# Binary cross-entropy with an 8-bit target: clip, negate and Ln by halves, and the last full store from GpSimd

## The chip, the cores and the metric

The kernel runs on one core of a Trainium2 chip. The metric is the device time of one execution in microseconds (us): the median of three runs before the change is 1889.43 us (1887.55 to 1890.08). One more execution was taken by the hardware profiler; it took 1891.86 us, and all rows below are from it.

The core's engines are called as in the profile: DVE (VectorE), ACT (ScalarE), POOL (GpSimd), SP (SyncE). TensorE does nothing here. Transfers between HBM and the on-chip memory run on 16 DMA engines, fed by queues of the engines that issue them.

## The reference

```python
"pred": np.random.uniform(0.01, 0.99, (8192, 8192)).astype(np.float32),
"target": np.random.randint(0, 2, (8192, 8192)).astype(np.float32),
...
eps = 1e-7
pred = np.clip(pred, eps, 1 - eps)
return -(target * np.log(pred) + (1 - target) * np.log(1 - pred))
```

Two inputs of 256 MiB are read and one of 256 MiB is written. Since the target is 0 or 1, the kernel computes the same with one logarithm: with p clipped, |t - 1 + p| is p where t is 1 and 1 - p where t is 0; the result is minus the Ln of it.

## The kernel before, in words

**Tiling.** The flat arrays are cut into chunks of 128 partitions by w columns: a first chunk of 8192 columns, 33 chunks of WIDE = 15232 columns, and a tail of three, a, b and c, of 6208, 6208 and 1024 columns. The last full chunk is called z (z = 33 when the first chunk is 0).

**Buffers.** `ring_p` holds three chunks of pred in float32; the result is computed in place there, so a slot is used again only when the store of its chunk has landed. `ring_t` has one slot only, in uint8: the target is cast from float32 to uint8 by the DMA that loads it. The next target can so be issued only when both halves of `merge` have read the present one. The tail's three chunks lie side by side in one slot of each ring.

**Steps for one chunk k.** `clip` (line 85, DVE): maximum and minimum with constants. `merge` (lines 91 and 94): DVE adds t - 1 to p, then ACT takes Abs. `log` (line 98, ACT): Ln. `negate` (line 102, DVE): times -1. Clips, merges and negates all stand in DVE's one queue, Abs and Ln in ACT's.

**DMA queues.** `load_p` (line 70) and `load_t` (line 73) are issued from GpSimd, except for the first p, which ACT issues. `store` (line 79) issues from GpSimd for chunks below z, and from SP for z, a, b and c. The store of c is cut into three by rows (108, 12, 8).

**Order.** The order is written out by hand (`manual_schedule`); within each engine's queue the instructions stand as in the source. A turn of the main loop for chunk k: merge in two halves, issue t of k+1, Ln, negate, clip of chunk k+1, store of k, issue p of k+2. So on GpSimd each turn has three issues: t (waits for the merges), store (waits for the negate), p (waits for the store that used the slot before). In the turn of chunk 1 alone, Ln and negate are by halves. After the loop come the merges of z with Ln by halves, the issue of all loads of a, b and c, and the rest of the tail, with clip and negate in the order of the source: negate z (half 0), clip a, negate z (half 1), store z, merge a, clip b, merge b, negate a, store a, clip c, merge c, negate b, store b, negate c, store c.

Of the kernel before, what the change touches and what calls it, by code (L numbers as in the profile page):

```python
# [1 line left out]

# [4 lines left out]

EPS = 1e-7

WIDE = 15232  # L10
SLOTS = 3
TAIL = (6208, 6208, 1024)
ROWS = (108, 12, 8)


@with_exitstack
def kernel(
    ctx: ExitStack,
    tc: tile.TileContext,
    pred: bass.AP,  # L20
    target: bass.AP,
    out: bass.AP,
):
    nc = tc.nc
    fp32 = mybir.dt.float32
    low = mybir.dt.uint8
    Alu = mybir.AluOpType
    Act = mybir.ActivationFunctionType
    P = nc.NUM_PARTITIONS

    R, C = pred.shape
    total = R * C // P
    rest = total - sum(TAIL)
    n = rest // WIDE
    first = rest - n * WIDE
    assert 0 < first <= WIDE and n > 4 and sum(TAIL) <= WIDE
    spots = [(first, 0)]
    spots += [(WIDE, k % SLOTS * WIDE) for k in range(1, n + 1)]
    c = (n + 1) % SLOTS * WIDE
    for w in TAIL:  # L40
        spots.append((w, c))
        c += w
    n = len(spots)
    z = n - 1 - len(TAIL)
    starts = [sum(w for w, _ in spots[:k]) * P for k in range(n)]

    pool = ctx.enter_context(tc.tile_pool(name="rings", bufs=1))
    ring_p = pool.tile([P, SLOTS * WIDE], fp32, name="ring_p", tag="ring_p")
    ring_t = pool.tile([P, WIDE], low, name="ring_t", tag="ring_t")
    warm = pool.tile([1, 8], fp32, name="warm", tag="warm")  # L50

    def chunk(ap, k):
        flat = ap.rearrange("r c -> (r c)")
        w = spots[k][0]
        return flat[starts[k] : starts[k] + w * P].rearrange("(p w) -> p w", p=P)

    def cols(ring, k, part, c):
        w = spots[k][0]
        i, m = part
        return ring[:, c + i * w // m : c + (i + 1) * w // m]  # L60

    def p_of(k, part=(0, 1)):
        return cols(ring_p, k, part, spots[k][1])

    def t_of(k, part=(0, 1)):
        return cols(ring_t, k, part, spots[k][1] % WIDE)

    def load_p(k):
        queue = nc.scalar if k == 0 else nc.gpsimd
        queue.dma_start(out=p_of(k), in_=chunk(pred, k))  # L70

    def load_t(k):
        nc.gpsimd.dma_start(out=t_of(k), in_=chunk(target, k))  # L73

    def store(k):
        queue = nc.sync if k >= z else nc.gpsimd
        r = 0
        for rows in ROWS if k == n - 1 else (P,):
            queue.dma_start(out=chunk(out, k)[r : r + rows, :], in_=p_of(k)[r : r + rows, :])  # L79
            r += rows  # L80
        assert r == P

    def clip(k, *part):
        p = p_of(k, *part)
        nc.vector.tensor_scalar(  # L85
            out=p, in0=p, scalar1=EPS, scalar2=1 - EPS, op0=Alu.max, op1=Alu.min
        )

    def merge(k, *part):
        p, t = p_of(k, *part), t_of(k, *part)  # L90
        nc.vector.scalar_tensor_tensor(  # L91
            out=p, in0=t, scalar=1.0, in1=p, op0=Alu.subtract, op1=Alu.add
        )
        nc.scalar.activation(out=p, in_=p, func=Act.Abs)  # L94

    def log(k, *part):
        p = p_of(k, *part)
        nc.scalar.activation(out=p, in_=p, func=Act.Ln)  # L98

    def negate(k, *part):  # L100
        p = p_of(k, *part)
        nc.vector.tensor_scalar(out=p, in0=p, scalar1=-1.0, scalar2=None, op0=Alu.mult)  # L102

    halves = (0, 2), (1, 2)
    with tc.manual_schedule():
        load_p(0)
        load_t(0)
        load_p(1)
        nc.vector.memset(warm, 1.0)  # L109
        nc.scalar.activation(out=warm, in_=warm, func=Act.Ln)  # L110
        clip(0)
        for k in range(z):
            for h in halves:
                merge(k, h)
                if k == 1:
                    log(k, h)
            load_t(k + 1)
            if k == 1:
                for h in halves:
                    negate(k, h)  # L120
            else:
                log(k)
                negate(k)
            clip(k + 1)
            store(k)
            if k + 2 <= z:
                load_p(k + 2)
        for h in halves:
            merge(z, h)
            log(z, h)  # L130
        a, b, c = range(z + 1, n)
        for j in a, b, c:
            load_p(j)
            load_t(j)
        negate(z, halves[0])
        clip(a)
        negate(z, halves[1])
        store(z)
        merge(a)
        log(a)  # L140
        clip(b)
        merge(b)
        log(b)
        negate(a)
        store(a)
        clip(c)
        merge(c)
        log(c)
        negate(b)
        store(b)  # L150
        negate(c)
        store(c)


# [1 line left out]
_INS = ['pred', 'target']  # L156
_OUTS = [((8192, 8192), 'float32')]


# [23 lines left out]
```

## Time and profile before

| | |
|---|---|
| median of three runs | 1889.43 us (1887.55 to 1890.08) |
| the profiled execution | 1891.86 us |
| its span (first to last instruction) | 1889.9 us |
| DVE busy | 1109.2 us (59%), 148 instructions |
| ACT busy | 897.3 us (47%), 112 instructions |
| POOL busy | 296.8 us (16%), 110 instructions |
| HBM read and written | 536.87 MB and 268.44 MB, 426 GB/s over the span |
| store, p and t of a full chunk, from issue to landing (median) | 28.3, 38.6 and 37.6 us |

The last row is the time that a transfer takes including its time in the queue. A row of the timeline has the start in us, the duration in us, the engine (with a q where it is the engine's sequencer that issues), the line, the operation, and in brackets the idle time before it with what ended it. In the stretches of the DMA share, each row has the stretch, its length, busy time and instructions of DVE, ACT and POOL, the granted TensorE clock, the busy share of the DMA engines and GB/s.

### The profile page before, as it was taken

What the parts mean: (1) busy time and instruction counts of PE and PEld (TensorE: products, weight loads), DVE (VectorE), ACT (ScalarE), POOL (GpSimd) and SP (SyncE); (2) the same over time, 40 slices, a digit from 0 to 9 for tenths busy, and PEclk for the clock granted to TensorE, in tenths of its full rate; (3) what the DMA queues carried; (4) which work ended last, traced back from release to release, by engine and by line L of the source; (5) the groups of instructions that cost most, each with busy time, mean ns of one, the idle gap of its engine ahead of it and who ended that gap; (6) DMA issues with size and microseconds to landing.
All of it is one profiled execution on the core that took longest, in us unless ns stands there. A gap on an engine that the chain in (4) does not pass through costs nothing.

```text
span 1889.9 us, 528 instructions
## 1 busy us (share of the span) xinstructions
DVE 1109.2 (59%) x148; ACT 897.3 (47%) x112; POOL 296.8 (16%) x110
## 2 busy tenths in 40 slices
DVE  3656655555666555456665555666555556665573
ACT  3553444555444455554444555444445554444564
POOL 0111111101111111011111101111111011111100
DMA  9999999999999999999999999999999999999997
GB/s 297 295 351 302 300 313 302 309 356 351 325 310 308 310 306 325 355 343 306 306 312 310 307 356 356 340 310 310 310 308 310 351 356 322 308 312 306 294 347 290
DMA packets 16003, 604.01 MB, mean 320 GB/s; under 512 B 1792, under 2 KB 1920, under 8 KB 2432
## 3 DMA queue, kind: packets, MB, share of 16 engines
q0 software_dynamic: 15264, 585.11, 97.1%
q1 hardware_dynamic: 592, 14.68, 1.8%
q10 hardware_dynamic: 144, 4.19, 0.6%
q14 instruction: 3, 0.02, 0.0%
HBM read 536.87 MB, written 268.44 MB: 426 GB/s over the span
## 4 chain that ended last, share of the span: by engine, by line
DMA 67%; issue 27%; DVE 3%; ACT 2%; POOL 0%; POOLq 0%; DVEq 0%
DMA ring_t<-in_target_dram 66%; DVE ring_p L91 2%; DMA ring_p<-in_pred_dram 1%; ACT ring_p L98 1%; ACT ring_p L94 1%; DVE ring_p L102 0%; POOL out_dram L79 0%; DVE ring_p L85 0%; DVEq L178 0%; POOL ring_p L70 0%; POOLq L73 0%; POOLq L79 0%; DVEq L91 0%
## 5 line engine op out<-in xcount | busy, mean ns | idle before, releaser
L94 ACT ACTIVATE ring_p<-ring_p 128x7616 f32<-128x7616 f32 (+3 forms) x71 | 451.3, 6356 | 976.5 <-DVE ring_p L91 976.5
L102 DVE TENSOR_SCALAR ring_p<-ring_p 128x15232 f32<-128x15232 f32 (+4 forms) x39 | 279.2, 7162 | 647.1 <-ACT ring_p L98 647.1
L91 DVE SCALAR_TENSOR_TENSOR ring_p<-ring_t,ring_p 128x7616 f32<-128x7616 uint8 (+3 forms) x71 | 554.3, 7847 | 101.6 <-DMA ring_t<-in_target_dram 101.5
L98 ACT ACTIVATE ring_p<-ring_p 128x15232 f32<-128x15232 f32 (+4 forms) x39 | 444.8, 11406 | 1.2
L79 POOL DMA_DIRECT2D out_dram<-ring_p x33 | 258.2, 7826 | 876.8 <-DVE ring_p L102 876.8
L85 DVE TENSOR_SCALAR ring_p<-ring_p 128x15232 f32<-128x15232 f32 (+3 forms) x37 | 278.7, 7533 | 19.5 <-DMA ring_p<-in_pred_dram 19.5
L73 POOL DMA_DIRECT2D ring_t<-in_target_dram x37 | 19.7, 532 | 638.9 <-DVE ring_p L91 638.1
L70 POOL DMA_DIRECT2D ring_p<-in_pred_dram x36 | 19.0, 528 | 0.0
L110 ACT ACT_TABLE_LOAD x1 | 1.3, 1283 | 1.1 <-PEq L167 1.1
L109 DVE MEMSET warm<- 1x8 f32 x1 | 0.1, 65 | 0.8 <-PEq L167 0.8
L110 ACT ACTIVATE warm<-warm 1x8 f32<-1x8 f32 x1 | 0.2, 207 | 0.0
L167 POOL MEMSET const-float32-0.0<- 128x1 f32 x1 | 0.1, 99 | 0.2 <-issue 0.2
L167 POOL MEMSET const-bfloat16-1.0<- 128x1 bf16 x1 | 0.1, 101 | 0.0
L167 POOL MEMSET const-float32-1.0<- 128x1 f32 x1 | 0.1, 98 | 0.0
L167 POOL MEMSET const-uint8-127<- 128x1 uint8 x1 | 0.1, 98 | 0.0
## 6 DMA issues: line engine op xcount, KB each, us to landing
ring_p<-in_pred_dram POOLq DMA_DIRECT2D x33, 7616.0 KB, 38.6
out_dram<-ring_p POOLq DMA_DIRECT2D x32, 7616.0 KB, 28.3
ring_t<-in_target_dram POOLq DMA_DIRECT2D x33, 1904.0 KB, 37.6
out_dram<-ring_p SPq DMA_DIRECT2D x1, 7616.0 KB, 28.2
ring_p<-in_pred_dram POOLq DMA_DIRECT2D x2, 3104.0 KB, 29.6
out_dram<-ring_p SPq DMA_DIRECT2D x2, 3104.0 KB, 9.1
ring_p<-in_pred_dram ACTq DMA_DIRECT2D x1, 4096.0 KB, 19.7
out_dram<-ring_p POOLq DMA_DIRECT2D x1, 4096.0 KB, 19.7
```

Source lines behind the costliest of these rows:

```text
L70: queue.dma_start(out=p_of(k), in_=chunk(pred, k))
L73: nc.gpsimd.dma_start(out=t_of(k), in_=chunk(target, k))
L79: queue.dma_start(out=chunk(out, k)[r : r + rows, :], in_=p_of(k)[r : r + rows, :])
L85: nc.vector.tensor_scalar(out=p, in0=p, scalar1=EPS, scalar2=1 - EPS, op0=Alu.max, op1=Alu.min)
L91: nc.vector.scalar_tensor_tensor(out=p, in0=t, scalar=1.0, in1=p, op0=Alu.subtract, op1=Alu.add)
L94: nc.scalar.activation(out=p, in_=p, func=Act.Abs)
L98: nc.scalar.activation(out=p, in_=p, func=Act.Ln)
L102: nc.vector.tensor_scalar(out=p, in0=p, scalar1=-1.0, scalar2=None, op0=Alu.mult)
L109: nc.vector.memset(warm, 1.0)
L110: nc.scalar.activation(out=warm, in_=warm, func=Act.Ln)
L167: nc = _bacc.Bacc("TRN2", target_bir_lowering=False, num_devices=1)
```

## The change

The function `log` goes; its Ln is now the last step of `merge`, so it is done right behind the Abs of the same piece: by halves in the loop, whole in the tail, where the pieces are whole. In the loop, negate and clip are called for each half in place of once for the chunk, for the first clip too. The order of the steps in the source is otherwise kept. In `store`, the test `k >= z` becomes `k > z`: the store of z is issued from GpSimd, behind all loads of the tail in its queue; a, b and c stay on SP.

```diff
     def store(k):
-        queue = nc.sync if k >= z else nc.gpsimd
+        queue = nc.sync if k > z else nc.gpsimd
...
         nc.scalar.activation(out=p, in_=p, func=Act.Abs)
-
-    def log(k, *part):
-        p = p_of(k, *part)
         nc.scalar.activation(out=p, in_=p, func=Act.Ln)
...
-        clip(0)
+        for h in halves:
+            clip(0, h)
         for k in range(z):
             for h in halves:
                 merge(k, h)
-                if k == 1:
-                    log(k, h)
             load_t(k + 1)
-            if k == 1:
-                for h in halves:
-                    negate(k, h)
-            else:
-                log(k)
-                negate(k)
-            clip(k + 1)
+            for h in halves:
+                negate(k, h)
+            for h in halves:
+                clip(k + 1, h)
             store(k)
...
         for h in halves:
             merge(z, h)
-            log(z, h)
...
         merge(a)
-        log(a)
         clip(b)
         merge(b)
-        log(b)
         negate(a)
         store(a)
         clip(c)
         merge(c)
-        log(c)
```

## The prediction

> **What bounds the kernel now.** First I read the page: engines, the slices of the span, the DMA queues.
>
> ```profile
> span 1889.9 us, 528 instructions
> DVE 1109.2 (59%) x148; ACT 897.3 (47%) x112; POOL 296.8 (16%) x110
> ...
> DMA  9999999999999999999999999999999999999997
> ...
> q0 software_dynamic: 15264, 585.11, 97.1%
> q1 hardware_dynamic: 592, 14.68, 1.8%
> ```
>
> No compute engine passes 59%. The 16 DMA engines are busy in every slice except the last, which shows 7 tenths: that slice (47 us) is the only place with DMA idle time worth having. So I went to the chain of waits in order of time, its last two turns of the loop and its end (start, length, what).
>
> ```profile
> 1702.33 37.52 DMA ring_t<-in_target_dram
> ...
> 1756.32 38.33 DMA ring_t<-in_target_dram
> ...
> 1811.13 45.51 DMA ring_t<-in_target_dram
> ...
> 1856.74 6.64 DVE ring_p L91
> 1863.40 5.39 ACT ring_p L94
> 1868.81 5.38 ACT ring_p L98
> 1874.21 3.40 DVE ring_p L102
> ```
>
> In the loop the chain is: t lands, two half merges (16.4 us), issue of the next t, 37.5 us to its landing. That looks like a latency loop, but the 37.5 us are queueing. Take the turn whose t landed at 1739.9: its store is issued at 1784.0, 44.0 after the landing, and lands 28.3 us later (median, DMA issues), at +72.3; p is issued at +51.8 and lands 38.6 later, at +90.4; t is issued at +16.4 and lands 37.6 later, at +54.0. Folded on the 54.0 us turn, store, p and t land at 18.3, 36.4 and 54.0: three transfers of 15232 columns, one after the other, about 18.1 us each, without a gap. The queue runs in the order of issue and is the bound. Every issue is early: the store by 10 us, p by 20, t by 20.
>
> At the end, 45.51 us for the small t of b, then DVE and ACT work with no DMA beside it. The timeline there (start, us, engine, line) and the DMA share by stretch:
>
> ```profile
> 1783.96 7.83 POOL L79 DMA_DIRECT2D out_dram<-ring_p  x1 [27.11 <-DVE ring_p L102]
> 1791.78 0.53 POOL L70 DMA_DIRECT2D ring_p<-in_pred_dram  x1
> ...
> 1803.13 0.53 POOL L73 DMA_DIRECT2D ring_t<-in_target_dram  x1 [10.83 <-DVE ring_p L91]
> ...
> 1833.21 47.79 SPq L79 DMA_DIRECT2D out_dram<-ring_p  x6
> ...
> 1856.74 6.63 DVE L91 SCALAR_TENSOR_TENSOR ring_p<-ring_t,ring_p 128x6208 f32<-128x6208 uint8 x1 [13.72 <-DMA ring_t<-in_target_dram]
> 1863.28 3.39 DVE L102 TENSOR_SCALAR ring_p<-ring_p 128x6208 f32<-128x6208 f32 x1
> ```
>
> ```profile
> 1862.40:1867.00 4.60, 4.60 (x3) 3.60 (x1) 0.00 (x0) 1.00 0.03 2
> 1867.00:1875.00 8.00, 2.28 (x3) 7.97 (x3) 0.00 (x0) 1.00 0.93 397
> 1875.00:1878.00 3.00, 3.00 (x2) 1.19 (x2) 0.00 (x0) 1.00 0.00 0
> 1878.00:1888.20 10.20, 0.21 (x1) 0.00 (x0) 0.00 (x0) 1.00 0.89 363
> ```
>
> SP issues the last full store (z) at 1833.21. It shares the DMA engines with the loads of b and c on the other queue, so t of b lands at 1856.7. DVE stands 13.72 us at merge(b), and behind that merge in DVE's order is negate(a) (1863.28), though a's Ln ended at 1850.5. So the stores of a and b go out late, and DMA is idle for 4.6 and 3.0 us (second last column: DMA share).
>
> **The change, part by part.**
>
> *Loop: clip, Ln and negate by halves.* Added: 34 clips, 32 negates, 32 Ln. A half of 7616 columns has rows: TENSOR_SCALAR 4127 ns against 8086 whole, so 2 x 4127 - 8086 = 0.17 us more for each; Ln 2 x 6549 - 12896 = 0.20 us more. Per turn DVE gains 0.34 us and ACT 0.20 us of work, on engines that are idle 40 to 50% of the turn. What moves, from t's landing: before, abs ends at 22.7, Ln (whole) at 35.6, negate at 43.7, store issued at 44.0, clip ends at 51.7. After: abs, Ln, abs, Ln of 6.55 each from 8.1 end at 34.3; negate of half 0 runs at 21.3 to 25.4, in DVE's idle time; negate of half 1 ends at 38.5, store issued at 38.8, clip halves end at 46.7. The store and the p behind it come some 5.2 us earlier. Counted on the chain this would be 32 x 5.2 = 166 us, but a store issued at 38.8 stands behind a t that fills the DMA engines until 54.0: its lead grows from 10 to 15 us and nothing else. t's issue stays at +16.4: negates and clips stand behind both merges. The order within GpSimd's queue (t, store, p) is the same. I cost it at 0; the cover is the 10 us and more of queued transfers. The new first wait, clip half 0 at 38.4 on its p (landed at 36.4), has 2 us to spare and 15 more before t's landing. At worst the issue of store and p (7.83 and 0.53 us on POOL) is held through both clip halves, to 46.7, still before today's 51.8. Bounds from rows: t takes 37.3 at the least, 37.7 median, 40.8 at most from issue to landing, and the turns average (1794.65 - 162.53)/30 = 54.40 us against 53.84 for the shortest; that 0.56 us per turn, 18 us over 33, is the jitter that other issue times might remove or double. I see no reason for either; 0 is the value of most turns.
>
> *Start.* clip(0) in halves: +0.1 to +0.2 us (4.43 us whole) ahead of merge(0), so t(1) is issued that much after 33.93. The p(1) ahead of it in the queue fills DMA to about 58.8 - 18.1 = 40.7: 6.8 us of cover, cost 0. Store(0) comes at about 46.6 instead of 49.10, needed at 58.8.
>
> *End: store z from GpSimd.* POOL has issued all loads of a, b, c by 1812.7, so nothing stands behind the store on its queue; SP loses it and has only the stores of a, b, c. Issue stays at about 1833.4, after negate(z). By columns (18.1 us for 15232): 6208 take 7.4, 1024 take 1.2. From the landing of store(z-1) (1783.96 + 28.7 = 1812.7) the queue holds four transfers of 7.4, two of 1.2, and z's 18.1: 50.1 us, to 1862.8; DMA fell silent at 1862.4, so this sum is sound. Moved to the same queue, the sum is the same and the order differs: t(b) lands at 1812.7 + 29.6 = 1842.3 instead of 1856.7, the loads end at 1844.7, z's store takes the DMA engines from there to 1862.8 if alone. Then: clip(b) to 1843.0, merge(b) to 1849.6 (6.62), negate(a) after a's Ln (1850.5), to 1853.9, store(a) on SP at 1854.2 instead of 1867; b's abs and Ln to 1861.3, negate(b) to 1864.7, store(b) at 1864.9 instead of 1878; c right behind. All three are queued while z and a still move (to 1862.4 + 8.0 = 1870), so DMA has no gap. Stores a, and b with c, took 8.0 and 10.2 us: the end of DMA is 1862.4 + 18.2 = 1880.6 instead of 1888.2: -7.6 us. Where a shares with z, its own gaps (0.93 share, 8.0 against 7.4) may be filled, up to -0.6 more. I take -7.9, the middle.
>
> *What sets the next end:* the stores of b and c, DMA-bound.
>
> The sum: the profiled execution took 1891.86 us (span 1889.9 and 1.96 around it), 2.43 above the median of the three runs. 1891.86 - 7.9 = 1884.0, on the median's footing 1889.43 - 7.9 = **1881.5 us**.
>
> **The rivals.**
>
> 1. *No change.* The order gains nothing, because z's store does not stay behind the loads, or because its issue on POOL is held. For it: POOL's store row takes 7.83 us and ends 0.1 after a TENSOR_SCALAR, against 0.53 otherwise. Against it: POOL's t issue at 1803.13 runs inside a merge in 0.53, and z's issue falls beside merge(a), an instruction of that kind; even held until clip(b) ends at 1843.0, it comes before the loads end at 1844.7. Held until negate(a) ends at 1853.9, DMA would stand 10.8 us and the time be 1881.5 + 10.8 = 1892.3. Time for this rival: 1889.4 (up to 1892.3). The Trainium skill speaks against this part of the change twice. "SBUF — State Buffer", section "SBUF: two separate sides", says that a GpSimd DMA cannot write its descriptors while VectorE is in a two-port mode, and advises a store from SP; the 7.83 against 0.53 agrees with the mechanism. "DMA: Bandwidth & Descriptors", section "Rules for kernel authors", says that spreading DMAs over issuing engines wins no bandwidth, by which alone a store moved between queues is worth nothing, 1889.4; the equal sum of 50.1 us agrees, and the idle 4.6 and 3.0 us are of order, not bandwidth.
>
> 2. *Half the gap stays.* b's chain (t, merge, abs, Ln, negate) becomes the bound if z and a are done before b's store comes. With z done at 1862.8 and a at 1866 at the earliest, b at 1864.9 leaves none; b late by 5 us would leave some 4: 1885.4.
>
> 3. *Slower: the loop's jitter grows.* Stores and p loads issued 5 us earlier hit t's transfer in another place, and each turn pays up to the 0.56 us again: +18 us, 1881.5 + 18 = 1899.5 at most. It decides from 7.9/33 = 0.24 us per turn. Against it: both are issued while t moves, as before.
>
> 4. *More gained:* that jitter goes: 1881.5 - 18 = 1863 at the least.
>
> **How the numbers follow.** Forecast 0.77; no change 0.09; half 0.04; slower 0.05; more gained 0.05. 0.2% is 3.8 us, about what can be told from no change here. Faster: 0.77 + 0.04 + 0.05 = 0.86; same 0.09; slower 0.05. The forecast's own bounds are -7.6 to -8.2, with runs that differ by 2.5 us: 1879 to 1884. The range takes in half the gap at its upper end: 1878.5 to 1886.
>
> **What would show it.** Right: the loop's turns still 54.4 us on average with stores issued 5 us earlier against t's landing; no store of z on SP; t(b)'s time to landing about 31 instead of 45.5; merge(b) near 1843; no stretch of idle DMA before the last store. DVE x214, ACT x144. Wrong: turns that average under 54.0 or over 54.7, z's issue long on POOL, idle DMA before the stores of a or b, or a t(b) that still lands near 1856.

## The result and the profile after

The changed kernel takes 1868.17 us (median of four runs, 1866.97 to 1868.90); the kernel before took 1888.49 us beside it (1887.12 to 1890.08). The ratio is 0.989, 95% interval 0.987 to 0.991: faster by 20 us, where 8 were forecast (1881.5, range 1878.5 to 1886). The profiled execution is the one of 1868.90 us, span 1867.1; before, it was the one of 1891.86, span 1889.9. The two spans are 22.8 us apart, the medians 20.3, so a term that is read off the two traces can be some 2.5 us larger than in the medians.

The page of the changed kernel: DMA engines still busy in every slice, and now nearly so in the last.

```profile
span 1867.1 us, 661 instructions
DVE 1116.7 (60%) x214; ACT 900.2 (48%) x144; POOL 282.8 (15%) x111
...
DMA  9999999999999999999999999999999999999998
...
q0 software_dynamic: 15408, 592.91, 98.6%
q1 hardware_dynamic: 448, 6.88, 0.9%
```

Its timeline at the last turn of the loop and in the tail (start, length, engine, line):

```profile
1766.42 3.86 POOL L79 DMA_DIRECT2D out_dram<-ring_p  x1 [21.82 <-DVE ring_p L99]
1770.27 4.05 POOL L70 DMA_DIRECT2D ring_p<-in_pred_dram  x1
1781.72 16.09 DVE L91 SCALAR_TENSOR_TENSOR ring_p<-ring_t,ring_p 128x7616 f32<-128x7616 uint8 x2 [7.53 <-DMA ring_t<-in_target_dram]
...
1820.46 0.54 POOL L79 DMA_DIRECT2D out_dram<-ring_p  x1 [20.76 <-DVE ring_p L99]
...
1830.03 6.63 DVE L91 SCALAR_TENSOR_TENSOR ring_p<-ring_t,ring_p 128x6208 f32<-128x6208 uint8 x1
1837.55 3.39 DVE L99 TENSOR_SCALAR ring_p<-ring_p 128x6208 f32<-128x6208 f32 x1 [0.89 <-ACT ring_p L95]
...
1840.97 14.35 SPq L79 DMA_DIRECT2D out_dram<-ring_p  x5
```

Split the span where t of z lands, the end of the loop: that was at 1794.7 us and is now at 1781.7. So the loop gained **13.0 us**, of which the forecast had none. From there to the end it was 95.2 us and is 85.4: the tail gained 9.8 us, of which the forecast had 7.9. In the tail merge(b) no longer waits (it stood 13.72 us), negate(a) comes 0.89 us behind it, and z's store was issued in 0.54 us. The DMA engines stay mostly busy there, where before they stood idle for 4.6 and 3.0 us:

```profile
1840.00:1850.00 10.00, 4.54 (x4) 9.94 (x4) 0.00 (x0) 1.00 0.89 382
1850.00:1856.00 6.00, 2.21 (x2) 0.22 (x1) 0.00 (x0) 1.00 0.85 364
1856.00:1862.00 6.00, 0.00 (x0) 0.00 (x0) 0.00 (x0) 1.00 0.96 380
```

The chain of waits (start, length, what) shows the same in the loop: every turn has one t from issue to landing, and late in the run nearly all take 37.3 to 37.6 us, where in the same part before they went from 37.5 to 39.0 (37.3 to 40.8 over the whole loop).

```profile
1636.24 37.41 DMA ring_t<-in_target_dram
...
1690.13 37.46 DMA ring_t<-in_target_dram
...
1744.07 37.56 DMA ring_t<-in_target_dram
```

That is the jitter of the fourth rival, and it went. The question for the experiments is why. The lines to look at are POOL's: the store row was 7.83 us long and is 3.86, and the p behind it went from 0.53 to 4.05. Counted from t's landing, the store's descriptors were all written at 51.9 before and are at 42.6 now; those of p at 52.4 before and 46.6 now.

### The profile page after: what moved, and what is told of

Its sections match the earlier page's. It is cut to its first block, busy times and chain, and to the rows that moved or that the text cites. A ratio compares the mean times of both kernels' runs of the same rounds, so it can differ in the third digit from the quotient of the medians.

```text
span 1867.1 us, 661 instructions
## 1 busy us (share of the span) xinstructions
DVE 1116.7 (60%) x214; ACT 900.2 (48%) x144; POOL 282.8 (15%) x111
## 4 chain that ended last, share of the span: by engine, by line
DMA 65%; issue 28%; ACT 4%; DVE 2%; POOL 0%; POOLq 0%; DVEq 0%; PEldq 0%
DMA ring_t<-in_target_dram 65%; ACT ring_p L95 2%; ACT ring_p L94 2%; DVE ring_p L91 1%; DVE ring_p L99 0%; POOL out_dram L79 0%; POOL ring_p L70 0%; DVEq L167 0%; POOLq L73 0%; POOLq L79 0%; DVEq L91 0%; PEldq L167 0%
## 5 line engine op out<-in xcount | busy, mean ns | idle before, releaser
L94 ACT ACTIVATE ring_p<-ring_p 128x7616 f32<-128x7616 f32 (+3 forms) x71 | 450.7, 6348 | 946.7 <-DVE ring_p L91 946.7
L99 DVE TENSOR_SCALAR ring_p<-ring_p 128x7616 f32<-128x7616 f32 (+3 forms) x71 | 284.3, 4006 | 475.8 <-ACT ring_p L95 475.8
L95 ACT ACTIVATE ring_p<-ring_p 128x7616 f32<-128x7616 f32 (+3 forms) x71 | 451.3, 6356 | 2.3
L85 DVE TENSOR_SCALAR ring_p<-ring_p 128x7616 f32<-128x7616 f32 (+3 forms) x71 | 281.3, 4003 | 19.2 <-DMA ring_p<-in_pred_dram 19.2
L79 POOL DMA_DIRECT2D out_dram<-ring_p x34 | 127.9, 3761 | 730.8 <-DVE ring_p L99 730.8
L70 POOL DMA_DIRECT2D ring_p<-in_pred_dram x36 | 135.3, 3759 | 0.0
## 6 DMA issues: line engine op xcount, KB each, us to landing
ring_t<-in_target_dram POOLq DMA_DIRECT2D x33, 1904.0 KB, 37.5
```

Of the source, the lines that this page charges most:

```text
L85: nc.vector.tensor_scalar(out=p, in0=p, scalar1=EPS, scalar2=1 - EPS, op0=Alu.max, op1=Alu.min)
```

## The experiments

**The theories.** L (late store): the end of POOL's row counts, not its start. Issue at 44.0 plus 7.83 at the clip is 51.9. The expectations below put the moment at which the store is wanted at about 52.3. The DMA packet records of the run before have it later: in the median turn the first of the 16 engines is through with t 1.2 us after the row's end and the last 1.85 us after it, and the landing at 54.0 is reported 0.4 us behind the last packet. So the lead was not 10 us but about 1.2, and L has it that engines that are through with t stand dry. S (skew) is L made sharper after the first runs: the 16 DMA engines drift apart, and the lead must cover that too. Against it: Q (the number of queues in use did it), A (Ln and negate by halves help by themselves), B (what hurts is GpSimd standing 7.8 us, at whatever time), T (the issue of the next t disturbs the store), P (the store's last packet is stretched when p is not yet in the queue as the store starts).

### The two parts alone

```diff
-        queue = nc.sync if k >= z else nc.gpsimd
+        queue = nc.sync if k > z else nc.gpsimd
```

> The kernel before with one edit: the store of z from GpSimd behind the loads of the tail. Theory L (late store): what the loop gained (t of z landed at 1781.6 instead of 1794.7, 13 us) comes from the halves, because the store's descriptors are written only when GpSimd gets past the whole clip (issue at 44.0 after t's landing, written by 51.8, wanted at about 52.3); the store of z gives the tail alone: 1888.5 - 9 = 1879.5, between 1878 and 1882, with t of z still landing near 1794. Rival Q (queue: the gain of the loop hangs on the number of queues in use): 1868 to 1871.

Measured: 1880.3 us beside 1889.8, ratio 0.9948 (0.9933 to 0.9964).

> The changed kernel with one edit undone: the store of z stays on SP. Theory L: the loop's 13 us without the tail's 9: 1875.5, between 1873 and 1878, t of z landing near 1782, and the idle stretches before the stores of a and b back. Rival Q: 1888.

This one is the changed kernel with that line put back:

```diff
-        queue = nc.sync if k > z else nc.gpsimd
+        queue = nc.sync if k >= z else nc.gpsimd
```

Measured: 1876.4 us, ratio 0.9931 (0.9916 to 0.9946). The merges of z and of b, in the timelines of the first and the second:

```profile
1790.94 16.09 DVE L91 SCALAR_TENSOR_TENSOR ring_p<-ring_t,ring_p 128x7616 f32<-128x7616 uint8 x2 [2.88 <-DMA ring_t<-in_target_dram]
...
1839.26 6.63 DVE L91 SCALAR_TENSOR_TENSOR ring_p<-ring_t,ring_p 128x6208 f32<-128x6208 uint8 x1
```

```profile
1780.37 16.09 DVE L91 SCALAR_TENSOR_TENSOR ring_p<-ring_t,ring_p 128x7616 f32<-128x7616 uint8 x2 [7.40 <-DMA ring_t<-in_target_dram]
...
1841.26 6.63 DVE L91 SCALAR_TENSOR_TENSOR ring_p<-ring_t,ring_p 128x6208 f32<-128x6208 uint8 x1 [12.61 <-DMA ring_t<-in_target_dram]
```

With z's store alone the loop ends at 1790.9, 3.8 us earlier than in the profiled execution before (single executions of before differ by 6 us here), and merge(b) has lost its wait; from t of z to the end it is 86.4 us (span 1877.3), 8.8 less than before. With the halves alone the loop ends at 1780.4 and merge(b) waits 12.61 us as before. Added up, the two parts give 1.2%, and the whole change 1.1% (0.9 to 1.3). Rival Q falls, since the loop gains with z's store still on SP.

### Which half of the loop's change

```diff
-            clip(k + 1)
+            for h in halves:
+                clip(k + 1, h)
```

> The kernel before with only the loop's clips by halves; Ln and negate whole, store of z on SP. The store is issued at 44.0 after t's landing as before, but GpSimd gets in after the first half of the clip, so its descriptors are written by about 48 instead of 51.8, some 4 us ahead of need. Theory L: nearly the whole gain of the loop, 1875 to 1878. Rival A (the shorter Ln and earlier negate on ACT and DVE matter, not GpSimd's wait): 1888.

Measured: 1889.0 us, ratio 0.9996 (0.9986 to 1.0005): nothing, against theory L. The rows were as expected, the result was not:

```profile
1563.77 3.86 POOL L79 DMA_DIRECT2D out_dram<-ring_p  x1 [27.11 <-DVE ring_p L102]
1567.62 4.05 POOL L70 DMA_DIRECT2D ring_p<-in_pred_dram  x1
...
1573.65 8.09 DVE L91 SCALAR_TENSOR_TENSOR ring_p<-ring_t,ring_p 128x7616 f32<-128x7616 uint8 x1 [2.10 <-DMA ring_t<-in_target_dram]
```

The store is written at 1567.63, 6 us ahead of this landing. But the trace's own DMA packet records show for this turn that 12 of the 16 engines began the store within 0.16 us of each other, at about the time it was written, while four were still moving t, the last for some 5 us more. The 12 had been through with t and stood dry, for up to 0.6 us. And the same 12 then took 3.0 to 3.3 us for their last packet of the store, where the usual is 2.25. In the first ten turns the engines were closer together (2.7 us at the tenth) and neither is seen. This is where theory S comes from.

```diff
             load_t(k + 1)
-            if k == 1:
-                for h in halves:
-                    negate(k, h)
-            else:
-                log(k)
-                negate(k)
+            for h in halves:
+                negate(k, h)
             clip(k + 1)
```

(Ln stands in `merge`, as in the changed kernel.)

> Ln and negate by halves as in the changed kernel, the loop's clips whole, store of z on SP. The store is issued at 38.8, held through the whole clip, written by about 46.7, some 5.5 us ahead of need. Theory L: nearly the whole gain of the loop, 1875 to 1878, with POOL's store row back at 7.83 us. Rival B (what hurt is GpSimd standing 7.8 us at the clip, at whatever time): 1888.

Measured: 1879.9 us (1879.3 to 1886.0), ratio 0.9945 (0.9928 to 0.9962): most of the gain, though 2 us short of the range. The profiled execution is the longest of the four, 1886.0.

```profile
760.02 16.09 DVE L91 SCALAR_TENSOR_TENSOR ring_p<-ring_t,ring_p 128x7616 f32<-128x7616 uint8 x2 [7.42 <-DMA ring_t<-in_target_dram]
...
798.75 7.83 POOL L79 DMA_DIRECT2D out_dram<-ring_p  x1 [21.81 <-DVE ring_p L99]
806.57 0.53 POOL L70 DMA_DIRECT2D ring_p<-in_pred_dram  x1
```

POOL stands its 7.83 us here too, from 38.7 to 46.6 after the landing, so rival B falls as far as most of the time goes: not the standing, but its end counts.

### The same halves, the store as late as with whole Ln

```diff
             for h in halves:
                 negate(k, h)
+            for again in (3, 4), (3, 4), (15, 16), (15, 16):
+                negate(k, again)
```

> The changed kernel with 5.2 us of DVE work behind negate (a quarter of half 1 negated twice more, its last eighth twice more): Ln, negate and clip by halves, but the store issued at 44.0 after t's landing and written by about 47.9, as in the run with the clips alone by halves. Theory S: a lead of some 4 us carries the early turns and fails once the DMA engines have drifted further apart than that; most of the loop's gain is lost, 1868 + 9 = 1877, between 1873 and 1881. Rival A (Ln and negate by halves help by themselves): 1868 to 1870.

Measured: 1886.3 us, ratio 0.9967 (0.9954 to 0.9980).

```profile
762.89 16.09 DVE L91 SCALAR_TENSOR_TENSOR ring_p<-ring_t,ring_p 128x7616 f32<-128x7616 uint8 x2 [2.17 <-DMA ring_t<-in_target_dram]
...
807.36 3.86 POOL L79 DMA_DIRECT2D out_dram<-ring_p  x1 [27.55 <-DVE ring_p L99]
811.21 4.05 POOL L70 DMA_DIRECT2D ring_p<-in_pred_dram  x1
```

The loss is larger than expected by 9 us. 5.8 us of it lie at the start, where the added work is on the path: the issue of t(3) comes at 128.3 instead of 122.5. From there to the issue of t(32) the turns average 54.37 us, the same as with the clips alone by halves (54.37) and against 54.05 for the changed kernel. Ln, negate and clip are all halved, and 0.13 of the 0.45 us a turn that the loop gained are left. Rival A falls.

### Whole Ln, negate and clip, the store early

```diff
+    def gap():
+        nc.vector.scalar_tensor_tensor(
+            out=idle, in0=idle, scalar=1.0, in1=idle, op0=Alu.subtract, op1=Alu.add
+        )
...
                 negate(k)
+            gap()
             clip(k + 1)
```

(`idle` is a spare tile of 1536 columns, set once at the start.)

> The kernel before with one DVE instruction of 1536 columns on a spare tile, of the kind of merge, between negate and clip in each turn: clips, Ln and negates stay whole, the store of z stays on SP, but GpSimd gets both the store and the p behind it written before the clip begins (44.6 and 45.1 instead of 51.8 and 52.4). Theory S: lead of some 7.5 us, nearly the whole loop gain, 1890 - 11 = 1879, between 1876 and 1881. Rival A: 1888 to 1891.

Measured: 1876.1 us (1875.8 to 1876.5), ratio 0.9912 (0.9897 to 0.9927): the gain of the halves (1876.4) with nothing halved that was not before, and 1.75 us of idle work added to each turn.

```profile
755.51 16.09 DVE L92 SCALAR_TENSOR_TENSOR ring_p<-ring_t,ring_p 128x7616 f32<-128x7616 uint8 x2 [0.74 <-DMA ring_t<-in_target_dram]
...
799.16 1.75 DVE L106 SCALAR_TENSOR_TENSOR idle<-idle 128x1536 f32<-128x1536 f32 x1
799.54 0.54 POOL L80 DMA_DIRECT2D out_dram<-ring_p  x1 [27.11 <-DVE ring_p L103]
800.07 0.53 POOL L71 DMA_DIRECT2D ring_p<-in_pred_dram  x1
800.83 8.09 DVE L86 TENSOR_SCALAR ring_p<-ring_p 128x15232 f32<-128x15232 f32 x1
```

The store is issued at 44.0 after the landing, exactly as in the kernel before, and this time takes 0.54 us, because the clip has not begun. This is the run that decides: what it shares with the changed kernel, and the kernel before has not, is that store and p are written early and that GpSimd no longer stands behind a whole clip; and the run with only Ln and negate by halves has most of the gain with that standing still in it. The mechanism behind the 7.83 us is the one that the Trainium skill gives on "SBUF — State Buffer" ("SBUF: two separate sides"): GpSimd can't write descriptors while VectorE is in a two-port mode. These rows agree, 0.54 us beside merge's kind of instruction and 7.83 beside a whole clip.

### The p alone late

```diff
             clip(k + 1)
+            if k + 2 <= z:
+                nc.vector.memset(p_of(k + 2, (0, 952)), 0.5)
             store(k)
```

This is added to the kernel with the gap. The memset writes 16 columns of the slot that the p load is about to fill, so the load must wait for it.

> The run with the gap before the clip (1876.1 us), and in each turn a DVE memset of 16 columns of the slot that the next p load fills, behind the clip: the store is still written at 44.6 after t's landing, but p only behind the clip, near 54, when the engines have begun the store and some 16 us before p's turn. No engine is held by another's port for it. Rival P (the store's last packet is stretched because p is not yet in the queue when the store starts): the time goes back towards 1887 and the stores' last packets are stretched again. Theory S (only engines that stood dry before the store lose time): 1876, between 1874 and 1879.

Measured: 1884.5 us (1877.4 to 1886.5, the profiled execution the longest of ten), ratio 0.9967 (0.9953 to 0.9980), between the two.

```profile
1562.31 0.54 POOL L80 DMA_DIRECT2D out_dram<-ring_p  x1 [27.11 <-DVE ring_p L103]
1572.00 0.53 POOL L71 DMA_DIRECT2D ring_p<-in_pred_dram  x1 [9.16 <-DVE ring_p L134]
1572.21 8.09 DVE L92 SCALAR_TENSOR_TENSOR ring_p<-ring_t,ring_p 128x7616 f32<-128x7616 uint8 x1 [0.51 <-DMA ring_t<-in_target_dram]
```

Neither theory has it right. In the first twenty turns p comes after the store has started, and no last packet of a store is stretched: P falls in its plain form. But the engines drift further apart than in any other run, up to 8.8 us, until the first of them is through with t at about the time when the store is written, 9.0 us ahead of the last; from then on packets are stretched. So the time at which p is written counts as well, some 16 us before its turn, through the drift. How is open: the run with only Ln and negate by halves has p written at 47.1 and drifts by 6.5 us.

### The issue of t

```diff
+            nc.gpsimd.memset(t_of(k, (3, 4)), 0.0)
             load_t(k + 1)
```

> The kernel before with a GpSimd memset of a quarter of t's slot ahead of each issue of t in the loop: t is issued some us later behind its merges, nothing else moves. In the trace before, the last of each store's eight packets per DMA engine is stretched (2.4 to 3.2 us instead of 2.25) at about the time when GpSimd issues t. Rival T (that issue stretches it): the store's last packets are back at 2.25 us and those of p behind it are stretched instead. Theory L: the store's last packets stay stretched, since the engines still start the store in step; time unchanged, 1886 to 1891.

Measured: 1890.0 us, ratio 1.0000 (0.9987 to 1.0012). t is issued some 3.4 us later:

```profile
1075.56 7.83 POOL L79 DMA_DIRECT2D out_dram<-ring_p  x1 [23.77 <-DVE ring_p L102]
...
1101.66 3.27 POOL L117 MEMSET ring_t<- 128x3808 uint8 x1 [17.76 <-DVE ring_p L91]
1105.23 0.53 POOL L73 DMA_DIRECT2D ring_t<-in_target_dram  x1 [0.30 <-POOL ring_t L117]
```

In this turn the store starts at 1083.4, when POOL's row ends, and its stretched last packets (0.81 us over the usual on the mean of 16 engines) are over by 1103.4 in the packet records, before t is issued. Rival T falls.

### Two delays that hit another chain

```diff
             for h in halves:
                 negate(k, h)
+            for again in halves[1], halves[1], (15, 16), (15, 16):
+                negate(k, again)
```

> The changed kernel with DVE work added behind negate: half 1 is negated twice more and its last eighth twice more, so the result is the same and the store is issued 9.4 us later, at 48.2 after t's landing; its descriptors are written by about 52.0, as late as before the change. Theory L: the loop's gain is lost, 1868 + 13 = 1881, between 1877 and 1885 (more if the store now starts late in every turn). Rivals A and B (short Ln, short waits of GpSimd): 1868 to 1870, since both stay as in the changed kernel.

Measured: 1941.6 us, ratio 1.027 (1.025 to 1.030).

```profile
733.05 16.07 DVE L91 SCALAR_TENSOR_TENSOR ring_p<-ring_t,ring_p 128x7616 f32<-128x7616 uint8 x2
...
781.08 8.16 DVE L85 TENSOR_SCALAR ring_p<-ring_p 128x7616 f32<-128x7616 f32 x2
781.46 3.86 POOL L79 DMA_DIRECT2D out_dram<-ring_p  x1 [31.52 <-DVE ring_p L99]
789.17 16.07 DVE L91 SCALAR_TENSOR_TENSOR ring_p<-ring_t,ring_p 128x7616 f32<-128x7616 uint8 x2
```

The expectation overlooked that the clips end later too. The merge follows the clip at once and waits for no DMA: the turn is now merge, Abs, Ln, negate, clip in a ring, 56.12 us long in every turn, and the DMA engines wait for it. It says nothing between the theories.

```diff
             if k + 2 <= z:
+                nc.gpsimd.memset(p_of(k + 2), 0.5)
                 load_p(k + 2)
```

> The changed kernel with a GpSimd memset of the whole slot between each store of the loop and the load of p behind it: the store's descriptors are written as early as in the changed kernel (42.7 after t's landing), those of p only at 55 to 62, after the engines have begun the store, but 8 us and more before p's turn (70). Theory S (what counts is the store's lead over the moment when the first of the 16 DMA engines is through with t; engines that stand dry start the store in a bunch and lose time again at its last packet): 1868 to 1871. Rival P (the last packet of the store is stretched because the p behind it is not yet in the queue when the store starts): back by 8 to 13 us, 1876 to 1881, with stretched last packets of the stores.

Measured: 2037.0 us, ratio 1.076 (1.074 to 1.078). The same ring, for another reason:

```profile
757.36 21.02 DVE L85 TENSOR_SCALAR ring_p<-ring_p 128x7616 f32<-128x7616 f32 x2
757.74 3.86 POOL L79 DMA_DIRECT2D out_dram<-ring_p  x1 [21.82 <-DVE ring_p L99]
761.59 12.81 POOL L120 MEMSET ring_p<- 128x15232 f32 x1
```

The memset gets in between the two halves of the clip, and the second half stands until it is over: two clips take 21.0 us instead of 8.2. This run says nothing between the theories either.

### All stores from SP, and the gap in the changed kernel

```diff
-        queue = nc.sync if k >= z else nc.gpsimd
+        queue = nc.sync
```

> The kernel before with all stores issued from SP: whole clips, Ln and negates. SP does not stand at the clip, so the store's descriptors are there at about 45, some 7 us ahead of need, but on a second queue: it shares the DMA engines with t from there on, and t lands later. Theory L: no more late store, the loop's gain comes, 1873 to 1879. If sharing between two queues, or t's later landing (the next t is issued 16.4 us behind it), costs DMA time in the loop: 1890 or more.

Measured: four runs of 1962.5, 1991.0, 1996.1 and 1996.9 us; the ratio of the two shorter ones to the kernel before is 1.046 (1.037 to 1.055). The waits of the profiled execution (the one of 1996.9 us; us in total, times, longest):

```profile
POOL ring_p L70 <- DMA out_dram<-ring_p: 480.4, 31, 24.5
```

SP does not stand at the clip, but on a second queue the store shares the engines with t and whatever comes behind it. Its median from issue to landing is 45.7 us (28.3 before), and the p that needs its slot waits for that landing, 480 us in 31 turns. "SBUF — State Buffer" of the Trainium skill ("SBUF: two separate sides") advises to issue from SP or ACT where VectorE shuts GpSimd out. Here that cost 4.6%: the store was written earlier, but lost its place in the one queue.

> The changed kernel with the same DVE instruction between its negates and clips: the store is written by 39.4 and p by 40, leads of 13 us and more. Theory S: the lead of the changed kernel is already longer than the drift of the engines (5 us at the end), so no change, 1866 to 1870. If the lead still pays beyond that: 1860 to 1865.

The edit, with the same `gap` as above, in the changed kernel:

```diff
             for h in halves:
                 negate(k, h)
+            gap()
             for h in halves:
                 clip(k + 1, h)
```

Measured: 1866.7 us (1866.5 to 1866.7), ratio 0.9862 (0.9847 to 0.9876). The changed kernel had 0.9891 (0.9874 to 0.9909) beside other runs of before; the intervals overlap, the medians are 1.5 us apart and the turns of the loop nearly equal (53.99 and 54.05), so a gain from a still longer lead is not shown.

### The runs side by side

Times after t's landing at which the store's and p's descriptors are all written; the mean turn from the issue of t(3) to that of t(32); from the DMA packet records the largest drift in a t (from the first engine's start to the last one's end, less 18.1 us) and the time that packets took over their usual 2.248 us (store and p) or 2.262 us (t), summed and divided by the 16 engines.

| run | store, p written | mean turn | largest drift | packets over usual: store and p, t |
|---|---|---|---|---|
| before | 51.9, 52.4 | 54.50 | 2.4 | 12.7, 1.4 |
| clips by halves | 47.9, 51.9 | 54.37 | 5.6 | 7.6, 5.3 |
| store at 44 | 48.3, 52.4 | 54.37 | 5.5 | 9.2, 5.3 |
| Ln, negate by halves | 46.6, 47.1 | 54.30 | 6.5 | 3.9, 5.1 |
| gap, p behind clip | 44.6, 54.3 | 54.23 | 8.8 | 4.2, 4.9 |
| halves alone | 42.6, 46.6 | 54.02 | 4.6 | 0.6, 2.0 |
| after | 42.6, 46.6 | 54.05 | 5.2 | 0.6, 2.9 |
| gap | 44.6, 45.1 | 53.95 | 4.2 | 0.7, 2.2 |
| after with gap | 39.3, 39.8 | 53.99 | 5.0 | 0.6, 2.3 |

The 0.45 us between the turns of before and after, times 29, is the 13 us. Each row is from one profiled execution.

Where was the 0.45 us lost? (The records do not name the engine; each engine's packets are strung together here by their times.) In those 29 turns before the change, the engines stood without a packet for 3.0 us (mean of 16), packets of store and p took 11.7 us over the usual and those of t 1.4: 16.2 us. After it, these are 0.1, 0.6 and 1.9: 2.6 us. The difference, 13.6, is the loop's 13.0 within 0.6, and most of it is stretched packets. So theory L as it was put, engines that stand dry, accounts for a fifth or so.

The stretching follows the lead all the same. Take as a turn's lead the time from the end of POOL's store row to the moment when the first engine is through with t. Its median is 1.2 us before the change, 6.8 after it and 4.9 with the gap. Sorted by it, 341 turns of eleven runs (31 each: the nine above, z's store alone, and the later issue of t) give:

| lead of the store, us | turns | store and p packets over usual, us a turn: mean (lowest to highest) |
|---|---|---|
| under 0.57 | 28 | 0.80 (0.65 to 0.97) |
| 0.57 to 1.0 | 21 | 0.56 (0.31 to 0.79) |
| 1.0 to 1.3 | 41 | 0.31 (0.11 to 0.56) |
| 1.3 to 1.6 | 61 | 0.09 (0.02 to 0.29) |
| over 1.6 | 190 | 0.02 (0.01 to 0.09) |

An engine that stands dry starts the store 0.57 us after the row's end, so only the first line has engines that wait. The relation holds within each run, whether the lead was short because the store was written late or because the engines had drifted. Starting together is not the cause: 13 turns have all engines through with t within 1 us of each other and a lead over 2.5 us, and none of them has more than 0.09 us.

## Why the prediction was wrong, step by step

- **What bounds the kernel: right, with one reading wrong.** The DMA queue is the bound and runs in order. But "Every issue is early: the store by 10 us" took the start of POOL's store row for the time when the store is in the queue. The row is 7.83 us long, and the prediction named it and its cause. Its end, 51.9, leaves 1.2 us in the median turn before the first engine is through with t, and less than nothing in some turns. This is the step that failed: a lead sized at 10 us of which about 1.2 us was there. And the three transfers did not come "without a gap" or at full pace: dry engines and stretched packets cost 16.2 us over 29 turns, 0.56 a turn, as much as it called jitter.
- **Loop at 0: wrong by 13.0 us** (halves alone: 1876.4 of 1889.8 us). The issue did move 5.2 us as worked out (38.7 after the landing, clips done at 46.6), and p cost nothing. The added work on DVE and ACT cost nothing either: the gap adds more and the time falls. What the step missed is that "the 10 us and more of queued transfers" were not there before, so there was something to gain: the lead grew from 1.2 to 6.8 us, where the prediction had 10 and 15.
- **Bounds of the jitter: right in size, wrong in the value taken.** The 0.56 us a turn, 18 us in all, held the answer (0.45 a turn); "I see no reason for either" was the judgement that failed. The chance of 0.05 for the fourth rival should have been the larger one, and the lower end of the range with it.
- **Start at 0:** t(1) is issued at 33.56 instead of 33.93; nothing is lost.
- **The tail: right, a little small.** -7.9 forecast; -8.8 with z's store alone, counted from t of z, -9.8 in the changed kernel. t(b) lands without a wait of merge(b), z's store takes 0.54 us on POOL, negate(a) and the stores of a and b come as worked out. The rival "no change" falls; most of DMA's idle time went, as the sum said.
- **Half the gap, and slower:** neither is seen in the changed kernel. More DVE work costs nothing as long as it is small (1.75 us a turn in the gap); 9.4 us of it behind negate turn the loop into a ring of 56.12 us.

## What to carry to other kernels

In this kernel a transfer from GpSimd was in its queue when GpSimd's row ended, not when it started. Count a lead from there to the moment when the data ahead of it is through on the first of the DMA engines; here a lead under 1.6 us cost time, also in turns in which no engine stood dry. Where GpSimd's store stands at a VectorE instruction, a small instruction of another kind between the two bought here what the reordering bought, and moving the store to another queue cost far more than the wait. A queue that looks busy in every slice still lost 0.7% to such late issues, since a stretched packet counts as busy; turns of unequal length were the sign.

## What the runs showed of the hardware that was not expected

- The 16 DMA engines of one queue drift apart by 4 to 5 us over 33 turns when the store is always written early, and turns average 53.95 to 54.05 us there, against 54.5 where late stores hold the engines together.
- When a store is written less than 1.6 us before the first engine needs it, packets of it, the last one above all, take longer: up to 3.4 us instead of 2.25, and 0.8 us on the mean of the engines at the shortest leads. Neither the issue of t nor a late p as such nor starting together explains it. What needs that lead, why it is the last packet, and why a p written late lets the drift grow to 8.8 us, stays open.
- The shut-out works both ways: a GpSimd memset of 12.8 us that came in between two halves of a clip held the second half for that long.
